# Weights of the accumulating DMAs read from HBM, a new order of the raw homes, and P2 ahead of P6 in the first pair of a chunk

## The chip, the cores and the metric

The kernel runs on one NeuronCore of a Trainium2 chip. The metric is the time of one execution on the device in microseconds (us), median over runs; the time before is 2619.73 us.

## The reference, cut to what matters

The reference is one step of a two-layer decoder on 512 prompt positions and 64 sample positions, 576 token columns in all. Each layer is a half-step SwiGLU FFN, a mixer (convolution, spatial gating, windowed attention, joined by `w_out`), and a second half-step FFN. The change lies in the four FFNs and in the edge between a mixer and the FFN behind it:

```python
def swiglu(x, w_gu, w_down):
    gu = x @ w_gu
    return (jax.nn.silu(gu[..., :D_FF]) * gu[..., D_FF:]) @ w_down

x = x + 0.5 * swiglu(rms_norm(x, n1), gu1, dn1)
m, conv_state, k_rows, v_rows, v_gmlp = token_mixer(rms_norm(x, nm), ...)
x = x + m
x = x + 0.5 * swiglu(rms_norm(x, n2), gu2, dn2)
```

`D_MODEL` is 1024 and `D_FF` is 2816, so the gate and the up matrix of an FFN have 22 column tiles of 128 each. Everything is float32.

## The kernel before, in words

**Precision.** Each weight block and each activation is split in a high part `h` (rounded to fp32r by a copy on ACT) and a rest `lo` = block - `h`. A product is three matmuls per 128 rows: `h` by high, `h` by low, `lo` by high. One matmul is 128x128 by 288 columns (half of the 576 tokens).

**A pair.** Column tile j of the gate and column tile j of the up matrix form a pair. It is computed from 2x2 blocks (`a11`, `a12` of the gate, `a21`, `a22` of the up matrix, each 128 x 512 numbers, 256 KB) by seven products instead of eight. The items of a pair are, by their number q in the code: 0 is P1 with `a11`, 1 is P5 with s0 = a21 + a22, 3 is P6 with s1 = s0 - a11, 2 is P2 with `a12`, 4 is P7 with s2 = a21 - a11, 5 is P3 with s3 = a12 - s1, 6 is P4 with `a22`. The four sums are made on DVE (`combine`, tile `sums`). A product has 12 matmuls (`product`, L563). P1, P6, P7 and P4 write the PSUM tile `c` (names `m` and `n` in turn), the others `z`. Behind P6 DVE adds `c` to a kept P5 (`z<-n,p`, L613), behind P7 it does so again (`u<-n,p`, L621); the next product that writes the same `c` waits for that read.

**Chunks.** An FFN works through its 22 pairs in four chunks; behind each chunk stand the down-projection matmuls of its pairs (`plain_ff` items, weights `w_dn`). The first pair of a chunk runs P1, P5, P6, P2 without work of an earlier pair between; in the later pairs the end of the pair before (P7, P3, P4) is mixed in. In the very first FFN three pairs are computed in plain form, so 85 pairs are left, in 16 chunks.

**The weight pipeline.** `load_raw` (L221) issues the load of a raw block on SP's queue, in order, into the next *raw home*: a list of ten homes (L227) is taken in rotation. `wr` has 4 buffers, `cb` has 4, `vT` and `ws` one each; tiles in `cb`, `vT` and `ws` carry the name `wc` in the rows. The mixer uses the `cb`, `vT` and `ws` storage for its own tiles, `cb` up to the last tile of `w_out`. A load waits until the block that had the home before has been read for the last time. `prepare` (L271) makes `h` and `lo` in a form buffer (eight, so the preparation of item i waits until PE has finished item i - 8); `advance` (L301) keeps the preparation seven items ahead of PE and the loads six items ahead of that. There are two ways. `by_vector` (L257): ACT copies `h`, DVE subtracts. `by_dma` (L263), used for `a11`, `a12` and `a22`, 255 times in all:

```python
        se.activation(out=h, in_=src, func=AF.Copy)
        se.activation(out=lo, in_=src, func=AF.Copy, scale=-1.0)
        ge.dma_start(out=lo.bitcast(F32), in_=src, accum_op=ALU.add)
```

Here ACT writes `h` and minus `h`, and an accumulating DMA, issued by POOL, adds the raw tile `src` to the second, so that `lo` = block - `h` without DVE. The raw tile is read by that DMA, and its home stays taken until the DMA has landed.

The order of the instructions on each engine is set by a scheduler when the program is built; at run time each engine's queue goes in order.

Of the kernel before, what the change touches and what calls it, by code (L numbers as in the profile page):

```python
# [9 lines left out]
F32 = mybir.dt.float32  # L10
F32R = mybir.dt.float32r
I32 = mybir.dt.int32
AF = mybir.ActivationFunctionType
ALU = mybir.AluOpType
# [81 lines left out]
def trunk(ctx: ExitStack, tc: tile.TileContext, a):  # L96
# [3 lines left out]
    ve, se, ge, sy = (_At(tc, e, HI) for e in (nc.vector, nc.scalar, nc.gpsimd, nc.sync))  # L100
# [29 lines left out]
    def ztile():  # L130
        return zp.tile([P, 2, 512], F32, tag="z", name="z")
# [30 lines left out]
    items = []  # L162

    def plain(ap, n, kind="plain", n0=0):
        for k0 in range(n0, n, 4):
            items.append((kind, ap[:, k0:min(k0 + 4, n), :], min(n - k0, 4)))

    def chunks(l, f):
        return CHUNKS0 if l == 0 and f == 0 else CHUNKS

    def ffn_items(l, f):
        j0 = N_PLAIN if l == 0 and f == 0 else 0
        gu = a["w_gu"][l, f]
        for j in range(j0):
            if j == 0:
                for n in (4, 8):
                    for h in range(2):
                        plain(gu[h], n, "plain_ff", n - 4)
            else:
                for h in range(2):  # L180
                    plain(gu[2 * j + h], 8, "plain_ff")
        for k0, k1 in chunks(l, f):
            last = None
            for j in range(max(k0, j0), k1):
                for i, q in ((j, 0), (j, 1)) if last is None else ((j, 1), (last, 4), (j, 0), (last, 5), (last, 6)):
                    items.append(("pair", (l, f, i), q))
                for q in (3, 2):
                    items.append(("pair", (l, f, j), q))
                last = j
            dn = [a["w_dn"][l, f, m, :, k0:k1, :] for m in range(KD)]  # L190
            for q in (4, 5):
                items.append(("pair", (l, f, last), q))
            plain(dn[0], 4, "plain_ff")
            items.append(("pair", (l, f, last), 6))
            plain(dn[1], 4, "plain_ff")
            plain(dn[0], k1 - k0, "plain_ff", 4)
            plain(dn[1], k1 - k0, "plain_ff", 4)
            for m in range(2, KD):
                plain(dn[m], k1 - k0, "plain_ff")
# [17 lines left out]
    state = {"load": 0, "prep": 0, "use": 0}  # L217
    state["form"] = state["raw"] = 0
    raws, ready = {}, {}

    def load_raw(i):  # L221
        kind, what, n = items[i]

        def raw(key, ap, n):
            home = "wr"
            if kind in ("pair", "plain_ff"):
                home = ("wr", "vT", "wr", "ws", "wr", "cb", "wr", "cb", "cb", "cb")[state["raw"] % 10]  # L227
                state["raw"] += 1
            if home == "wr":
                t = wp.tile([P, 4 * P], F32, tag="wr", name="wr", bufs=4)  # L230
            elif home == "cb":
                t = sp.tile([P, CB], F32, tag="cb", name="wc", bufs=4)
            else:
                t = sp.tile([P, 640 if home == "vT" else 768], F32, tag=home, name="wc")
            t = t[:, 0:n * P].rearrange("p (k m) -> p k m", k=n)
            sy.dma_start(out=t, in_=ap)
            raws[key] = t

        if kind != "pair":
            raw(i, what, n)  # L240
        else:
            l, f, j = what
            for h, k in {0: ((0, 0),), 1: ((1, 0), (1, 4)), 2: ((0, 4),)}.get(n, ()):
                raw((what, h, k), a["w_gu"][l, f, 2 * j + h, :, k:k + 4, :], 4)

    def parts(ff, n):
        tag = "w"
        if ff:
            tag = ("sp", "w", "pt", "w")[state["form"] % 4]
            state["form"] += 1  # L250
        if tag == "w":
            f = wp.tile([P, 2, 4, P], F32R, tag="w", name="w", bufs=4)
        else:
            f = big(tag, "w", F32R).rearrange("p (a k m) -> p a k m", a=2, k=4)
        return f[:, 0, 0:n, :], f[:, 1, 0:n, :]
# [4 lines left out]
        ve.tensor_tensor(out=lo, in0=src, in1=h.bitcast(F32), op=ALU.subtract)  # L260
        return h, lo, n

    def by_dma(src, n):  # L263

        h, lo = parts(True, n)
        se.activation(out=h, in_=src, func=AF.Copy)
        se.activation(out=lo, in_=src, func=AF.Copy, scale=-1.0)
        ge.dma_start(out=lo.bitcast(F32), in_=src, accum_op=ALU.add)
        return h, lo, n

    def prepare(i):  # L271
        kind, what, n = items[i]
        if kind != "pair":
            ready[i] = by_vector(raws.pop(i), n, kind != "plain")
            return

        a11, a12, a21, a22 = (raws.get((what, h, k)) for h, k in ((0, 0), (0, 4), (1, 0), (1, 4)))
        s = state["sums"]

        def combine(q, x, y, op):  # L280
            ve.tensor_tensor(out=s[:, q], in0=x, in1=y, op=op)

        if n == 0:
            r = by_dma(a11, 4)
        elif n == 1:
            combine(0, a21, a22, ALU.add)
            r = by_vector(s[:, 0], 4)
        elif n == 3:
            combine(1, s[:, 0], a11, ALU.subtract)
            r = by_vector(s[:, 1], 4)  # L290
            combine(2, a21, a11, ALU.subtract)
        elif n == 2:
            r = by_dma(a12, 4)
            combine(3, a12, s[:, 1], ALU.subtract)
        elif n == 6:
            r = by_dma(a22, 4)
        else:
            r = by_vector(s[:, n - 2], 4)
        ready[what, n] = r
# [273 lines left out]
    def ffn(l, f, nxt):  # L573
        start = l == 0 and f == 0
        p5s = slot("e", "p5").rearrange("p (i n) -> p i n", i=2)
        r = None
        for k0, k1 in chunks(l, f):
# [32 lines left out]
            def p6(o):  # L610

                product(o["c"], weights(o["what"], 3), fac["b"][3], False)
                ve.tensor_tensor(out=o["z"][:, 1, h1], in0=o["c"], in1=o["p5"], op=ALU.add)  # L613

            def p2(o):
                product(o["z"][:, 0, h1], weights(o["what"], 2), fac["b"][2], False)
# [54 lines left out]
            last = None  # L671
            for j in range(k0, k1):
                if start and j < N_PLAIN:
                    plainly(j)
                    continue
                o = {"what": (l, f, j), "z": ztile(), "c": mtile("n" if j % 2 else "m")[:, h1], "p5": p5s[:, j % 2, h1]}
                if last is None:
                    p1(o)
                    p5(o)
                    seed(o)  # L680
                    save(o)
                else:
                    p5(o)
                    save(o)
                    p7(last)
                    p1(o)
                    seed(o)
                    p3(last)
                    p4(last)
                p6(o)  # L690
                p2(o)
                if r is None:
                    r = rms()
                last = o
# [575 lines left out]
```

## Time and profile before

| | us |
|---|---|
| median of 3 runs | 2619.73 (2618.04 to 2623.62) |
| profiled execution, its own time | 2623.66 |
| profiled execution, span from first to last instruction | 2621.9 |
| PE busy | 2584.4 (99%) |
| DVE busy | 1909.9 (73%) |
| ACT busy | 1273.5 (49%) |
| POOL busy | 286.9 (11%) |

The mean granted TensorE clock of the span is 0.995. The DMA queues moved 303.30 MB, of it 66.86 MB by the accumulating DMAs of POOL; HBM read is 221.43 MB, 88 GB/s over the span.

How to read it: busy time of PE includes the overlap of pipelined matmuls, so a stretch in which PE is busy throughout is one in which a matmul starts every 132 ns; the number of matmuls in a stretch tells how much of it was lost. An engine's instructions go in order, so one that waits holds all that stand behind it.

### The profile page before, as it was taken

To read this page: it belongs to the slowest core of one execution; us is meant where nothing else is said; L and a number is where in the kernel's file an instruction comes from. 1 tells how busy PE (TensorE), PEld (TensorE's weight loads), DVE (VectorE), ACT (ScalarE), POOL (GpSimd) and SP (SyncE) were. 2 spreads that over 40 slices of the span, in tenths; PEclk is the share of its full clock that TensorE was granted. 3 is DMA by queue.
4 is the path that set the end of the run, shared out by engine and by line. 5 is a ranking of instruction groups with operands and counts; after the bars stand their busy time and mean duration, and the time that the engine had idled before them with its cause. 6 is when DMAs were issued, how large, how long until landed. Compare 5 with 4: busy or idle time off the path is not lost.

```text
span 2621.9 us, 49387 instructions
## 1 busy us (share of the span) xinstructions
PE 2584.4 (99%) x18996; PEld 2519.7 (96%) x18996; DVE 1909.9 (73%) x3488; ACT 1273.5 (49%) x2415; POOL 286.9 (11%) x317
## 2 busy tenths in 40 slices
PE   8999999999999999999999999999999999999999
PEld 8999999988899999999999999998989999999999
DVE  8676665688897786766885766747988977756665
ACT  6455453335424564554674554532453245644543
POOL 0111010010010021111110111101100100111110
PEclk9999999999999999999999999999999999999999
DMA  6565454231222464655564655533212234655553
GB/s 178 129 147 130 123 121 129 84 88 58 67 83 81 131 151 124 147 124 131 132 136 119 149 125 132 141 103 85 78 57 73 85 104 123 142 126 137 126 135 95
DMA packets 193920, 303.30 MB, mean 116 GB/s; under 512 B 39434, under 2 KB 56714, under 8 KB 193684
## 3 DMA queue, kind: packets, MB, share of 16 engines
q1 hardware_dynamic: 156820, 233.28, 29.5%
q0 software_dynamic: 36720, 66.86, 15.2%
q8 instruction: 149, 2.44, 0.4%
q14 instruction: 87, 0.71, 0.1%
q10 hardware_dynamic: 144, 0.00, 0.0%
HBM read 221.43 MB, written 8.84 MB: 88 GB/s over the span
## 4 chain that ended last, share of the span: by engine, by line
PE 91%; DVE 3%; DMA 3%; issue 1%; ACT 1%; SPq 0%; POOL 0%; DVEq 0%; POOLq 0%; ACTq 0%
PE z L322 18%; PE z L325 17%; PE z L328 17%; PE z L569 14%; PE n L569 9%; PE m L569 9%; PE n L86 4%; PE m L86 2%; DMA wc<-w_gu 2%; DMA w<-wc 1%; DVE w L88 1%; ACT w L88 1%; DVE u L88 0%; DVE sums L88 0%; DVE x L88 0%
## 5 line engine op out<-in xcount | busy, mean ns | idle before, releaser
L88 ACT ACTIVATE w<-wr 128x512 fp32r<-128x512 f32 (+1 forms) x533 | 324.0, 622 | 657.9 <-PE z L328 526.2
L569 PE MATMUL z<-xh,w 128*128 128x288 f32 x2040 | 443.4, 299 | 5.5 <-DVE z L88 3.7
L88 ACT ACTIVATE w<-wc 128x512 fp32r<-128x512 f32 (+2 forms) x509 | 271.5, 565 | 243.3 <-PE z L328 89.1
L88 DVE TENSOR_TENSOR w<-sums,w 128x512 fp32r<-128x512 f32 x340 | 234.1, 689 | 198.5 <-ACT w L88 194.7
L569 PEld LDWEIGHTS z<-xh,w 128*128 128x128 f32 x2040 | 337.5, 188 | 11.8 <-DVE z L88 5.8
L322 PE MATMUL z<-xh,w 128*128 128x288 f32 x1520 | 337.4, 303 | 8.0 <-ACT w L88 6.6
L88 DVE TENSOR_TENSOR w<-wr,w 128x512 fp32r<-128x512 f32 (+2 forms) x373 | 254.3, 682 | 122.0 <-ACT w L88 121.5
L325 PE MATMUL z<-xl,w 128*128 128x288 f32 x1520 | 328.0, 297 | 0.0
L328 PE MATMUL z<-xh,w 128*128 128x288 f32 x1520 | 327.7, 296 | 0.0
L322 PE MATMUL z<-ah,w 128*128 128x288 f32 x1408 | 303.6, 296 | 0.4
L325 PE MATMUL z<-al,w 128*128 128x288 f32 x1408 | 302.1, 296 | 0.6 <-DVE al L88 0.5
L328 PE MATMUL z<-ah,w 128*128 128x288 f32 x1408 | 301.3, 296 | 0.0
L569 PE MATMUL z<-xl,w 128*128 128x288 f32 x1020 | 300.5, 295 | 0.0
L88 ACT ACTIVATE w<-sums 128x512 fp32r<-128x512 f32 x340 | 212.1, 624 | 176.3 <-PE z L569 90.4
L322 PEld LDWEIGHTS z<-xh,w 128*128 128x128 f32 x1520 | 245.6, 191 | 22.1 <-issue 11.7
L325 PEld LDWEIGHTS z<-xl,w 128*128 128x128 f32 x1520 | 248.2, 191 | 0.7 <-issue 0.7
L328 PEld LDWEIGHTS z<-xh,w 128*128 128x128 f32 x1520 | 246.7, 190 | 0.5 <-issue 0.3
L88 DVE SCALAR_TENSOR_TENSOR c<-cb,vec,c 128x512 f32<-128x512 f32 x480 | 244.5, 556 | 0.2
L322 PEld LDWEIGHTS z<-ah,w 128*128 128x128 f32 x1408 | 226.7, 189 | 2.6 <-DVE x L88 2.3
L325 PEld LDWEIGHTS z<-al,w 128*128 128x128 f32 x1408 | 226.6, 189 | 1.8 <-DVE al L88 1.8
L328 PEld LDWEIGHTS z<-ah,w 128*128 128x128 f32 x1408 | 226.6, 189 | 0.0
L88 POOL DMA_DIRECT2D w<-wc x175 | 150.5, 860 | 616.6 <-ACT w L88 221.3
(255 smaller groups left out, 4854.5 us busy)
## 6 DMA issues: line engine op xcount, KB each, us to landing
wc<-w_gu SPq DMA_DIRECT2D x212, 256.0 KB, 2.9
wr<-w_in SPq DMA_DIRECT2D x184, 256.0 KB, 2.8
w<-wc POOLq DMA_DIRECT2D x175, 256.0 KB, 3.7
wr<-w_gu SPq DMA_DIRECT2D x140, 256.0 KB, 2.8
wr<-w_dn SPq DMA_DIRECT2D x92, 256.0 KB, 2.8
w<-wr POOLq DMA_DIRECT2D x80, 256.0 KB, 4.1
wc<-w_dn SPq DMA_DIRECT2D x36, 256.0 KB, 3.0
wr<-w_out SPq DMA_DIRECT2D x32, 256.0 KB, 3.2
```

Source lines behind the costliest of these rows:

```text
L86: r = f(*args, **kw)
L88: r = f(*args, **kw)
L322: pe.matmul(out=z[c], lhsT=wh, rhs=rh[:, s], start=first, stop=False)
L325: pe.matmul(out=z[c], lhsT=wh, rhs=rl[:, s], start=False, stop=False)
L328: e = pe.matmul(out=z[c], lhsT=wl, rhs=rh[:, s], start=False, stop=last)
L569: e = pe.matmul(out=out, lhsT=w[:, k, :], rhs=r, start=first and k == 0 and i == 0, stop=k == n - 1 and i == 2, skip_group_check=True)
```

## The change

Three things, and one that follows from them.

1. `by_dma` gets a third argument, the block in HBM, and the accumulating DMA reads that instead of the raw tile. The raw tile is then read by the two ACT copies (and by `combine`), no longer by the DMA.
2. The list of raw homes has two `wr` in positions 4 and 5 and the four `cb` at its end, and the rotation starts again at each `w_out` tile of a mixer, so that the FFN behind a mixer begins with `wr`, `vT`, `wr`, `ws`, `wr`, `wr`.
3. In the first pair of a chunk P2 comes ahead of P6, in the list of items and in the program; s3 is made in the preparation of P6 (item 3) instead of P2 (item 2). `a12` is loaded with item 3 in the later pairs, an item earlier than before. In the first pair of a chunk the key of the load list is 2 for the item behind P5 and 3 for the other, so the condition holds for both: `a12` is loaded twice there, 16 loads of 256 KB more on SP's queue in the whole program (P2's two copies read the later one).

```diff
@@ -184,7 +184,7 @@
             for j in range(max(k0, j0), k1):
                 for i, q in ((j, 0), (j, 1)) if last is None else ((j, 1), (last, 4), (j, 0), (last, 5), (last, 6)):
                     items.append(("pair", (l, f, i), q))
-                for q in (3, 2):
+                for q in (2, 3) if last is None else (3, 2):
                     items.append(("pair", (l, f, j), q))
                 last = j
             dn = [a["w_dn"][l, f, m, :, k0:k1, :] for m in range(KD)]
@@ -218,13 +218,17 @@
     state["form"] = state["raw"] = 0
     raws, ready = {}, {}
 
+    def block(what, h, k):
+        l, f, j = what
+        return a["w_gu"][l, f, 2 * j + h, :, k:k + 4, :]
+
     def load_raw(i):
         kind, what, n = items[i]
 
         def raw(key, ap, n):
             home = "wr"
             if kind in ("pair", "plain_ff"):
-                home = ("wr", "vT", "wr", "ws", "wr", "cb", "wr", "cb", "cb", "cb")[state["raw"] % 10]
+                home = ("wr", "vT", "wr", "ws", "wr", "wr", "cb", "cb", "cb", "cb")[state["raw"] % 10]
                 state["raw"] += 1
             if home == "wr":
                 t = wp.tile([P, 4 * P], F32, tag="wr", name="wr", bufs=4)
@@ -236,12 +240,13 @@
             sy.dma_start(out=t, in_=ap)
             raws[key] = t
 
+        if kind == "plain_out":
+            state["raw"] = 0
         if kind != "pair":
             raw(i, what, n)
         else:
-            l, f, j = what
-            for h, k in {0: ((0, 0),), 1: ((1, 0), (1, 4)), 2: ((0, 4),)}.get(n, ()):
-                raw((what, h, k), a["w_gu"][l, f, 2 * j + h, :, k:k + 4, :], 4)
+            for h, k in {0: ((0, 0),), 1: ((1, 0), (1, 4)), (2 if items[i - 1][2] == 1 else 3): ((0, 4),)}.get(n, ()):
+                raw((what, h, k), block(what, h, k), 4)
 
     def parts(ff, n):
         tag = "w"
@@ -260,12 +265,12 @@
         ve.tensor_tensor(out=lo, in0=src, in1=h.bitcast(F32), op=ALU.subtract)
         return h, lo, n
 
-    def by_dma(src, n):
+    def by_dma(src, n, hbm):
 
         h, lo = parts(True, n)
         se.activation(out=h, in_=src, func=AF.Copy)
         se.activation(out=lo, in_=src, func=AF.Copy, scale=-1.0)
-        ge.dma_start(out=lo.bitcast(F32), in_=src, accum_op=ALU.add)
+        ge.dma_start(out=lo, in_=hbm.bitcast(F32R), accum_op=ALU.add)
         return h, lo, n
 
     def prepare(i):
@@ -281,7 +286,7 @@
             ve.tensor_tensor(out=s[:, q], in0=x, in1=y, op=op)
 
         if n == 0:
-            r = by_dma(a11, 4)
+            r = by_dma(a11, 4, block(what, 0, 0))
         elif n == 1:
             combine(0, a21, a22, ALU.add)
             r = by_vector(s[:, 0], 4)
@@ -289,11 +294,11 @@
             combine(1, s[:, 0], a11, ALU.subtract)
             r = by_vector(s[:, 1], 4)
             combine(2, a21, a11, ALU.subtract)
+            combine(3, a12, s[:, 1], ALU.subtract)
         elif n == 2:
-            r = by_dma(a12, 4)
-            combine(3, a12, s[:, 1], ALU.subtract)
+            r = by_dma(a12, 4, block(what, 0, 4))
         elif n == 6:
-            r = by_dma(a22, 4)
+            r = by_dma(a22, 4, block(what, 1, 4))
         else:
             r = by_vector(s[:, n - 2], 4)
         ready[what, n] = r
@@ -687,8 +692,12 @@
                     seed(o)
                     p3(last)
                     p4(last)
-                p6(o)
-                p2(o)
+                if last is None:
+                    p2(o)
+                    p6(o)
+                else:
+                    p6(o)
+                    p2(o)
                 if r is None:
                     r = rms()
                 last = o
```

On POOL the 255 accumulating DMAs, which alternated between `w<-wr` and `w<-wc`, all read `w_gu` now. Their number and their place among POOL's other work stay. Three places show what else moves.

DVE in the first pair of the third chunk of the first FFN: `sums<-...` are the four combinations, `w<-sums,w` a subtraction of `by_vector`, `z<-n,p` and `u<-n,p` the reads of `c` behind P6 and P7. Before:

```order
L88 TENSOR_TENSOR sums<-wc,sums 128x512
L88 TENSOR_TENSOR w<-sums,w 128x512
L88 TENSOR_TENSOR sums<-sums,wr 128x512
L88 TENSOR_TENSOR z<-n,p_185 128x288
L88 TENSOR_TENSOR w<-sums,w 128x512
L88 TENSOR_TENSOR sums<-wc 128x512
L88 TENSOR_TENSOR w<-sums,w 128x512
L88 TENSOR_TENSOR u<-n,p_185 128x288
```

With the change:

```order
L88 TENSOR_TENSOR sums<-wc,sums 128x512
L88 TENSOR_TENSOR w<-sums,w 128x512
L88 TENSOR_TENSOR sums<-sums,wc 128x512
L88 TENSOR_TENSOR z<-n,p_185 128x288
L88 TENSOR_TENSOR w<-sums,w 128x512
L88 TENSOR_TENSOR sums<-wc,wr 128x512
L88 TENSOR_TENSOR w<-sums,w 128x512
L88 TENSOR_TENSOR u<-n,p_185 128x288
```

The combination that stands ahead of `u<-n,p` is the first sum of a later pair in both; its two raw blocks lay in two `wc` homes, now in a `wc` (the `vT` home) and a `wr`.

SP at the start of the last FFN, behind the mixer of the second layer: the last loads of `w_out`, then the FFN's own. Before:

```order
L88 DMA wr<-w_out 128x512 x4
L88 DMA wr<-w_gu 128x512 x4
L88 DMA wc<-w_gu 128x512 x5
L88 DMA wr<-w_gu 128x512
L88 DMA wc<-w_gu 128x512
L88 DMA wr<-w_gu 128x512 x2
L88 DMA wc<-w_gu 128x512 x2
L88 DMA wr<-w_gu 128x512 x2
```

With the change:

```order
L88 DMA wr<-w_out 128x512 x4
L88 DMA wr<-w_gu 128x512 x3
L88 DMA wc<-w_gu 128x512
L88 DMA wr<-w_gu 128x512 x3
L88 DMA wc<-w_gu 128x512 x4
L88 DMA wr<-w_gu 128x512
L88 DMA wc<-w_gu 128x512
L88 DMA wr<-w_gu 128x512
```

Four loads for `wr` and five for `wc` (the first of them into `cb`) stood in a row; now three for `wr`, one for `wc` (the `vT` home), three for `wr` and then four for `wc`.

PE in the first pair of a chunk, from the end of P6 to the start of P7 (`n<-fh` and `n<-fl` are both; the `z` rows between are other products). Before, in which 9 more `z` rows follow ahead of the first `n<-fh` of P7:

```order
L569 MATMUL n<-fh,w 128x288
L569 MATMUL z<-xl_81,w 128x288
L569 MATMUL z<-xh_73,w 128x288
L569 MATMUL z<-xh_74,w 128x288
L569 MATMUL z<-xl_82,w 128x288
L569 MATMUL z<-xh_74,w 128x288
L569 MATMUL z<-xh_75,w 128x288
L569 MATMUL z<-xh_76,w 128x288
L569 MATMUL z<-xl_84,w 128x288
L569 MATMUL z<-xh_76,w 128x288
L569 MATMUL z<-xh_77,w 128x288
L569 MATMUL z<-xl_85,w 128x288
```

With the change, up to the start of P7:

```order
L574 MATMUL n<-fh,w 128x288
L574 MATMUL z<-xl_81,w 128x288
L574 MATMUL z<-xh_73,w 128x288
L574 MATMUL z<-xh_74,w 128x288
L574 MATMUL z<-xl_82,w 128x288
L574 MATMUL z<-xh_74,w 128x288
L574 MATMUL z<-xh_75,w 128x288
L574 MATMUL z<-xl_83,w 128x288
L574 MATMUL z<-xh_75,w 128x288
L574 MATMUL n<-fh,w 128x288
```

Between the last matmul of P6 and the first of P7 stood 20 matmuls, now 8; the 12 of P2 stand between the two halves of P6 instead.

## Rows read from the trace of the kernel before

**Rows 1.** What PE waited for in the whole span: total us, times, longest.

```profile
PE z L569 <- DVE z L88: 3.7, 8, 0.6
...
PE m L569 <- ACT z L88: 1.2, 1, 1.2
```

**Rows 2.** What SP's queue waited for in the whole span: total us, times, longest.

```profile
SPq L88 <- DMA w<-wc: 532.3, 173, 11.1
SPq L88 <- DMA w<-wr: 322.5, 77, 10.6
```

**Rows 3.** Stretches: PE, PEld, DVE, ACT, POOL busy (instructions); granted clock, DMA share, GB/s.

```profile
260.00:300.00 40.00, 40.00 (x303) 39.89 (x302) 28.30 (x50) 19.90 (x37) 3.44 (x4) 1.00 0.56 142
...
217.00:240.00 23.00, 22.17 (x163) 21.45 (x163) 14.09 (x24) 13.64 (x26) 5.16 (x6) 1.00 0.67 145
326.00:345.00 19.00, 17.26 (x116) 16.77 (x116) 10.62 (x20) 9.81 (x19) 3.44 (x4) 0.91 0.68 142
920.00:944.00 24.00, 22.00 (x161) 20.89 (x161) 20.66 (x48) 16.56 (x34) 5.19 (x7) 1.00 0.64 153
...
2212.00:2242.00 30.00, 25.54 (x184) 24.02 (x183) 25.82 (x57) 20.33 (x40) 5.99 (x7) 1.00 0.66 163
2340.00:2351.00 11.00, 10.16 (x75) 9.69 (x74) 8.68 (x16) 6.62 (x12) 2.58 (x3) 1.00 0.75 166
2448.00:2459.00 11.00, 10.09 (x74) 9.62 (x73) 8.44 (x15) 6.43 (x12) 2.58 (x3) 1.00 0.74 168
```

**Rows 4.** Chain that ended last, third chunk's start: start us, us, what.

```profile
220.76 4.68 DMA w<-wc
225.50 3.60 DMA wc<-w_gu
```

**Rows 5.** DVE's timeline there: start, us, instruction, [idle before <- releaser].

```profile
223.28 0.47 DVE L88 TENSOR_TENSOR z<-n,p 128x288 f32<-128x288 f32 x1
226.35 0.69 DVE L88 TENSOR_TENSOR w<-sums,w 128x512 fp32r<-128x512 f32 x1 [2.60 <-ACT w L88]
229.18 0.69 DVE L88 TENSOR_TENSOR sums<-wc 128x512 f32<-128x512 f32 x1 [2.14 <-DMA wc<-w_gu]
...
230.39 0.45 DVE L88 TENSOR_TENSOR u<-n,p 128x288 f32<-128x288 f32 x1
```

**Rows 6.** ACT's timeline there, the two copies of `a22`.

```profile
219.31 1.15 ACT L88 ACTIVATE w<-wc 128x512 fp32r<-128x512 f32 x2 [0.93 <-PE n L569]
```

**Rows 7.** PE's timeline there: P6's end, P7's start, P4's start.

```profile
222.88 0.29 PE L569 MATMUL n<-fh,w 128*128 128x288 f32 x1
...
225.75 0.29 PE L569 MATMUL n<-fh,w 128*128 128x288 f32 x1
...
230.90 0.66 PE L569 MATMUL n<-f,w 128*128 128x288 f32 x3 [0.23 <-DVE u L88]
```

**Rows 8.** Chain that ended last, fourth chunk's start.

```profile
327.92 4.66 DMA w<-wc
...
332.64 5.15 DMA wc<-w_gu
...
339.58 2.41 PE n L569 x12
```

**Rows 9.** DVE's timeline there.

```profile
337.87 0.69 DVE L88 TENSOR_TENSOR sums<-wc 128x512 f32<-128x512 f32 x1 [3.66 <-DMA wc<-w_gu]
```

**Rows 10.** SP's and PE's timelines at the last FFN's start.

```profile
2210.64 5.10 SPq L88 DMA_DIRECT2D wc<-w_gu  x5
...
2221.11 0.40 PE L569 MATMUL n<-xh,w 128*128 128x288 f32 x1 [1.48 <-ACT w L88]
...
2225.53 0.54 PE L569 MATMUL n<-xh,w 128*128 128x288 f32 x2 [1.46 <-DMA w<-wr]
```

**Rows 11.** DVE's timeline at the start of the FFN behind the first mixer.

```profile
920.30 0.69 DVE L88 TENSOR_TENSOR sums<-wr,wc 128x512 f32<-128x512 f32 x1 [1.25 <-DMA wc<-w_gu]
```

**Rows 12.** DMA issues by the page: KB each, median us from issue to landing.

```profile
wc<-w_gu SPq DMA_DIRECT2D x212, 256.0 KB, 2.9
...
w<-wc POOLq DMA_DIRECT2D x175, 256.0 KB, 3.7
```

## The prediction

> **What bounds the kernel now.** I begin with the stretches [rows 3]. In the undisturbed one, from 260 to 300 us, PE starts 303 matmuls in 40.00 us, one each 0.132 us, while DVE (28.30 us) and ACT (19.90 us) have room. That is the bound for nearly the whole span, and no part of this change takes a matmul away: the time can fall only by what PE stands still. How much a stretch loses is its length less its matmuls times 0.132 us. From 217 to 240 us that is 23.00 - 163 x 0.132 = 1.48 us, from 326 to 345 us 19.00 - 116 x 0.132 = 3.69 us, from 2340 to 2351 us 1.10 us, from 2448 to 2459 us 1.23 us, and at the starts of the two FFNs behind a mixer 2.75 us (920 to 944) and 5.71 us (2212 to 2242). These six places together are 15.96 us, some 0.6% of the time; the edges of a stretch make each uncertain by a matmul.
>
> Next, who makes PE wait at a chunk's start. The chain of waits of the third chunk [rows 4] has the accumulating DMA from 220.76 us for 4.68 us, and behind it at once, at 225.50 us, a load of the next raw blocks for 3.60 us. DVE's timeline [rows 5] shows what hangs on it: the combination that needs those blocks starts at 229.18 us after 2.14 us of waiting, and `u<-n,p`, which needs nothing of it but stands behind it, only at 230.39 us. P4 writes the `c` that this reads, so PE starts it at 230.90 us [rows 7]. The load waited for a home that the accumulating DMA was still reading, though ACT had made both its copies from 219.31 us in 1.15 us [rows 6]. The fourth chunk repeats it a size larger: accumulation 4.66 us, load 5.15 us [rows 8], DVE waits 3.66 us [rows 9], and then P4 takes 2.41 us for its 12 matmuls instead of 12 x 0.132 = 1.58, under a mean granted clock of 0.91 in that stretch [rows 3], which is a part of it at 1.2 instead of 2.4 GHz after PE had stood still. In the whole span SP's queue waited 532.3 and 322.5 us for accumulating DMAs [rows 2]; little of that reaches PE, but PE's waits for DVE's `z` sum to 3.7 us in 8 places [rows 1], at just these starts.
>
> **The change part by part.** *The DMA reads HBM.* A home comes free when ACT has copied: at 219.31 + 1.15 = 220.46 us, where it was 225.50 us, some 5.0 us earlier. The load then lands near 220.5 + 3.6 = 224.1 us, and the combination, which stands behind a subtraction that ends at 226.35 + 0.69 = 227.04 us [rows 5], finds its blocks there. `u<-n,p` can then start when P7 has ended, 12 matmuls after 225.75 us [rows 7], near 227.7 us, well before P4's turn. What is late next is the subtraction that waits for ACT, 2.60 us at 226.35 us [rows 5], but it is over before P7 ends. So the four starts go: 1.48 + 3.69 + 1.10 + 1.23 = 7.5 us, the half clock included; two smaller ones of the kind I leave out. I take 7.4 of it, bounds 4 (only the waits that DVE is named for [rows 1, 7]) and 8.
>
> The accumulating DMA itself: the trace has none with HBM as its source. Its price lies between that of a plain load, 2.9 us, and 3.7 us plus the 2.25 us that a slowed load took more (5.15 against 2.9) [rows 8, 12]. I take 3.7, as before, since it moves as many bytes into the same tile. The one at 220.76 us landed at 225.44 us and PE used its form at 230.90 us: 5.4 us to spare, so neither end reaches PE in the steady work. The cover fails only at the first products of an FFN.
>
> The Trainium skill speaks against this part: its page "HBM Reference", section "Latency", gives 0.2 us for an access on average and 2 us under high load. By that page, as an estimate, an accumulation would land up to 2 us later than from on-chip memory; no run here shows it yet. It would add 2 us at each of the two places where an accumulation holds PE at an FFN's start, so the sum below would be 4 us smaller.
>
> *The homes.* Behind the mixer the first pair had its blocks in `cb` homes that the mixer held to its end: the load row at 2210.64 us is 5.10 us long for five issues [rows 10], and DVE waits 1.25 us for such a load at 920.30 us [rows 11]. Now the first six blocks have `wr`, `vT` and `ws`. Of the last FFN's loss of 5.71 us the 1.48 us at 2221.11 us and the 1.46 us at 2225.53 us [rows 10] go, and of the rest (the DVE that has fallen behind) I count 1.1 us: 4.0. Of the first layer's 2.75 us I count 1.3, by the ACT wait of 1.2 us [rows 1] that follows on the DVE wait. The rest of both belongs to the residual stream's own preparation and stays. Together 5.3, bounds 0 and 8.46. The FFNs that stand behind another FFN or at the program's beginning get no earlier homes: 0.
>
> *P2 ahead of P6.* DVE's `z<-n,p` starts 0.40 us after the start of P6's last matmul (222.88 to 223.28 us [rows 5, 7]), and PE could use `c` some 0.51 us later (230.39 to 230.90 us, the same kind of read). So P7 may follow 0.91 us after that start. With 20 matmuls between it came 21 x 0.132 = 2.77 us later, with 8 it comes 1.19 us later: 0.28 us is left. A DVE instruction of 0.69 us in front of it would cost 0.41 us, at most 6.6 us over 16 first pairs; where DVE is idle, as here, nothing. I take 1.0 us. That P2 and the load of `a12` move by an item costs nothing: seven items of look-ahead cover it.
>
> *The second load of `a12`.* 16 more loads of 2.9 us [rows 12] on a queue that waits hundreds of microseconds anyway: 0, with 16 x 0.33 us of issue as the worst, off PE's path.
>
> *The program's beginning.* The scheduler sets a subtraction of 0.69 us ahead of a small chain that PE waits for in the first FFN's normalisation. I take 1.0 us of loss, bounds 0 and 1.4 (two of them).
>
> Sum: -7.4 - 5.3 + 1.0 + 1.0 = -10.7 us. From the profiled execution's 2623.66 us that is 2613.0; this execution stands 3.9 us above the median of the runs, so the median comes to 2609 us. With the bounds of the terms the likeliest case reaches from about 2602 (-16.5 us of gain, no loss, and some scatter of the runs) to 2616 (gains of 4 and 3, losses of 1.4 and 2).
>
> **The rivals.** *The earlier loads collide.* Loads that are freed by ACT's copies start within a microsecond or two of POOL's accumulating DMA; the row of 5.15 us shows a load stretched by such company [rows 8]. At the fourth chunk it would still land at 327.9 + 5.15 = 333.1 us, ahead of the 337.87 - 3.66 = 334.2 us at which DVE wanted it, so the chunk starts keep their gain. The FFN starts, where the loads come one behind the other, would not: 5.3 us are lost again, 2614.3 us. The Trainium skill, "DMA: Bandwidth & Descriptors", section "Issuing engines are not separate DMA queues", says that transfers of sync and gpsimd run on the same 16 engines and interleave; this trace agrees with it by that row.
>
> *Accumulations from HBM land later.* Were they later by the 2.25 us of the stretched load, two FFN starts would pay it: 4.5 us, 2613.6 us. For it: nothing but the longer way. Against it: the loads, which come from HBM, land sooner (2.9 us) than the accumulations (3.7 us) [rows 12].
>
> *Slower: DVE is late for P7.* If the combinations go on waiting for loads, now in front of `z<-n,p`, then a wait such as the 2.14 us [rows 5] no longer lies under 20 matmuls: P7 starts 2.14 - 0.28 = 1.86 us late at 16 first pairs, 29.8 us, against 10.7 of gain: 2638.8 us. It decides against the change once DVE is late by about 1.3 us on average (16 x 1.0 us = 10.7 + 5.3). Against it: DVE had been idle at that point in the rows, for some 2 us on each side.
>
> *The waits only change their name.* DVE's queue stands behind another late block or subtraction at the same starts; then PE gains nothing it can keep, 2619.7 us.
>
> **How the numbers follow.** The likeliest case has 0.60, the later accumulations 0.10, the collision 0.12, DVE late for P7 0.09, waits that only change their name 0.09. About 0.2%, 5.2 us, is what a measurement of this kernel can tell from no change: faster means below 2614.5, slower above 2625.0. The collision, at 2614.3, counts half. Faster: 0.60 + 0.10 + 0.06 = 0.76; same 0.06 + 0.09 = 0.15; slower 0.09. The range goes from 2602 to 2618: it leaves out the two last rivals, 0.18, and takes in the others with their scatter.
>
> **What would show it.** In the profile of the changed kernel SP's queue should no longer wait for accumulating DMAs. At the third and fourth chunk's start DVE should start its combination without waiting for a load, `u<-n,p` right behind P7, and the granted clock from 326 to 345 us should be 1.00. The matmuls counted in the six stretches should come out at 0.132 us each, except for some 1.5 us at each FFN behind a mixer. The forecast is wrong if `w<-w_gu` takes over 5.9 us to land, if PE waits at P7 for DVE's `z` at many chunk starts, or if the loads behind the mixer still begin late.

## The result, and the profile after

The changed kernel takes 2603.64 us (median of 4 runs, 2601.36 to 2607.47), the kernel before 2620.32 us beside it (4 runs, 2618.04 to 2623.62): a ratio of 0.9937, 95% interval 0.9920 to 0.9954. The forecast was 2609 us, range 2602 to 2618. Run a second time beside other kernels, the same program took 2606.52 us against 2619.44, ratio 0.9951 (0.9938 to 0.9963), so the gain lies near 13 to 17 us. The profiled execution took 2607.47 us; its span is 2605.7 us, 16.2 us less than that of before. What is read from HBM rises from 221.43 to 292.47 MB, 116 GB/s over the span.

The same seven stretches as in [rows 3], moved by as much as their place in the program had moved, in the profile of the changed kernel (PE, PEld, DVE, ACT and POOL busy with their instructions, granted clock, DMA share, GB/s):

```profile
260.00:300.00 40.00, 40.00 (x302) 39.83 (x301) 29.10 (x51) 20.20 (x38) 4.31 (x5) 1.00 0.57 135
219.70:242.70 23.00, 23.00 (x174) 22.77 (x173) 15.67 (x27) 14.63 (x28) 5.17 (x6) 1.00 0.72 157
327.40:346.40 19.00, 19.00 (x143) 18.77 (x142) 12.41 (x22) 11.89 (x24) 4.32 (x5) 1.00 0.77 164
916.00:940.00 24.00, 23.40 (x174) 22.61 (x173) 20.98 (x49) 17.19 (x34) 5.17 (x6) 1.00 0.67 148
2200.40:2230.40 30.00, 29.58 (x221) 28.78 (x220) 25.84 (x57) 20.56 (x40) 5.14 (x6) 1.00 0.58 140
2327.70:2338.70 11.00, 11.00 (x85) 10.97 (x84) 8.54 (x16) 6.93 (x14) 2.59 (x3) 1.00 0.87 175
2434.30:2445.30 11.00, 11.00 (x84) 10.97 (x84) 8.50 (x16) 7.41 (x14) 2.59 (x3) 1.00 0.84 179
```

Where PE stood still before it now starts a matmul every 0.132 us: 174 in 23.00 us (163 before), 143 in 19.00 us (116), 85 and 84 in 11.00 us (75 and 74), all at a granted clock of 1.00, also in the stretch that had 0.91. The starts behind a mixer lose 24.00 - 174 x 0.132 = 1.03 us and 30.00 - 221 x 0.132 = 0.83 us where it was 2.75 and 5.71.

SP's queue waits, summed over the span of the changed kernel (total us, times, longest):

```profile
SPq L88 <- DVE w L88: 943.4, 445, 5.5
SPq L88 <- ACT w L88: 493.4, 210, 9.7
SPq L88 <- DVE sums L88: 360.8, 85, 15.7
```

No accumulating DMA is left among them [rows 2]; ACT's copies and DVE's combinations release the homes. DVE's timeline in the first pair of the third chunk shows what follows [rows 5]:

```profile
227.62 0.47 DVE L88 TENSOR_TENSOR z<-n,p 128x288 f32<-128x288 f32 x1 [1.66 <-PE n L574]
228.46 0.69 DVE L88 TENSOR_TENSOR w<-sums,w 128x512 fp32r<-128x512 f32 x1 [0.37 <-ACT w L88]
229.18 0.69 DVE L88 TENSOR_TENSOR sums<-wc,wr 128x512 f32<-128x512 f32 x1
229.79 0.68 DVE L88 TENSOR_TENSOR w<-sums,w 128x512 fp32r<-128x512 f32 x1
230.39 0.45 DVE L88 TENSOR_TENSOR u<-n,p 128x288 f32<-128x288 f32 x1
```

The combination at 229.18 us waits for no load, and `u<-n,p` stands right behind the end of P7. PE's and SP's timelines beside it:

```profile
227.22 0.29 PE L574 MATMUL n<-fh,w 128*128 128x288 f32 x1
...
228.41 0.30 PE L574 MATMUL n<-fh,w 128*128 128x288 f32 x1
...
2203.16 2.72 SPq L88 DMA_DIRECT2D wc<-w_gu  x4
```

The first two are P6's last matmul and P7's first: 1.19 us apart, and DVE's read of `c` began 0.40 us after the one and was over before the other, as worked out ahead. The third is the last FFN's loads into `cb`: four issues in 2.72 us at 2203.16 us, which no first product needs any more [rows 10].

Where the 16.2 us of span came from is read from DVE's 144 instructions `x<-z,x`, which end every chunk and every mixer. Between them the span falls into pieces that have the same work in all kernels of this study. "Start" is up to the end of the very first chunk, "chunks" are the other 15 up to their last `x<-z,x`, "FFN behind mixer" runs from a mixer's first `x<-z,x` to its last (the first pair of the next FFN lies in it), "attention" runs from the first to the last gate product `gz<-z,rstd` of a mixer, and the rest of the mixers is alike in all to 0.3 us. Each column is the difference to the profile of before, in us:

| profiled kernel | start | 15 chunks | FFN behind mixer | attention |
|---|---|---|---|---|
| the change | +3.47 | -10.67 | -5.16 | -3.68 |
| the change, once more | +2.58 | -12.06 | -5.20 | -3.32 |
| HBM as source alone | +0.64 | -8.43 | -0.23 | -6.14 |
| raw homes alone | -1.70 | -1.57 | -6.81 | -5.42 |
| P2 ahead of P6 alone | +1.06 | -1.76 | +3.30 | -5.78 |
| a12 loaded once | +0.79 | -10.61 | -6.80 | -6.31 |
| HBM source, home held | -0.66 | +9.77 | -0.46 | -3.39 |
| HBM source and homes | +3.40 | -11.95 | -6.80 | -3.05 |
| old order in first chunk | +1.86 | -12.95 | -6.80 | -5.65 |
| old order in first chunks | +3.52 | -12.61 | -6.79 | -4.54 |
| source and homes, tile at start | +1.29 | -12.87 | -6.80 | -3.94 |
| old order and tile at start | -1.52 | -10.09 | -6.81 | -4.05 |

The column "FFN behind mixer" repeats to 0.1 us between kernels that share the homes and have no second load of `a12`; "chunks" lies between -10.1 and -13.0 us in all eight profiles with source and homes. "Attention" does not repeat, and it is lower in every other profile, though none of the kernels changes the mixers' code. It is a property of the one execution, most of all of the profiled one of before, which stood 3.9 us above its median.

A good part of what does not repeat in "start" and "chunks" is TensorE's granted clock. In the profile of before it is below 1.00 once in the 15 chunks, in the fourth chunk, in the stretch that [rows 3] give with 0.91:

```profile
338.00:348.00 10.00, 8.42 (x52) 8.42 (x53) 8.42 (x15) 4.31 (x8) 1.72 (x2) 0.83 0.69 160
```

Ten us at 0.83 are a part at 1.2 instead of 2.4 GHz; they lose up to 10 x (1 - 0.83) = 1.7 us of matmuls, as an estimate (counted in matmuls, two such places below lose 1.3 and 1.5 us). The profile with the homes alone has the same fall at the same place, both of the change have one in the third FFN instead, several have none in the chunks, and that with the home held has three. Without these stretches (at 1.7 us each, so roughly) the eight profiles with source and homes lie at -10.1 to -12.1 us in the chunks, HBM alone at -8.4, the homes alone at -1.6, the order alone at -0.1 and the held home at +6.4.

### The profile page after: what moved, and what is told of

Read it like the earlier page. It is cut to its first block, busy times and chain, and to the rows that moved or that the text cites. A ratio compares the mean times of both kernels' runs of the same rounds, so it can differ in the third digit from the quotient of the medians.

```text
span 2605.7 us, 49108 instructions
## 1 busy us (share of the span) xinstructions
PE 2577.6 (99%) x18996; PEld 2519.0 (97%) x18996; DVE 1910.9 (73%) x3488; ACT 1272.8 (49%) x2415; POOL 291.3 (11%) x317
## 3 DMA queue, kind: packets, MB, share of 16 engines
HBM read 292.47 MB, written 8.84 MB: 116 GB/s over the span
## 4 chain that ended last, share of the span: by engine, by line
PE 94%; DVE 3%; DMA 1%; ACT 1%; issue 1%; POOL 0%; SPq 0%; DVEq 0%; POOLq 0%; ACTq 0%
PE z L327 18%; PE z L330 17%; PE z L333 17%; PE z L574 15%; PE n L574 10%; PE m L574 10%; PE n L86 4%; PE m L86 2%; DVE w L88 1%; ACT w L88 0%; DVE x L88 0%; DMA rt<-q 0%; DMA wr<-w_gu 0%; DVE c L88 0%; DVE sums L88 0%
## 5 line engine op out<-in xcount | busy, mean ns | idle before, releaser
L88 ACT ACTIVATE w<-wr 128x512 fp32r<-128x512 f32 (+2 forms) x575 | 337.8, 604 | 625.7 <-PE z L333 487.7
L88 ACT ACTIVATE w<-wc 128x512 fp32r<-128x512 f32 (+2 forms) x467 | 257.8, 583 | 303.2 <-PE z L333 133.1
L88 POOL DMA_DIRECT2D w<-w_gu x255 | 220.2, 864 | 1507.3 <-ACT w L88 980.7
L88 DVE TENSOR_TENSOR w<-wr,w 128x512 fp32r<-128x512 f32 (+2 forms) x373 | 240.6, 645 | 82.6 <-ACT w L88 81.6
L327 PEld LDWEIGHTS z<-xh,w 128*128 128x128 f32 x1520 | 245.5, 191 | 22.2 <-issue 11.7
```

Source lines behind the costliest of these rows:

```text
L88: r = f(*args, **kw)
L327: pe.matmul(out=z[c], lhsT=wh, rhs=rh[:, s], start=first, stop=False)
```

## The experiments

**HBM as the source alone.** Accumulating DMAs as in the change, everything else as before.

```diff
+    def block(what, h, k):
...
-        ge.dma_start(out=lo.bitcast(F32), in_=src, accum_op=ALU.add)
+        ge.dma_start(out=lo, in_=hbm.bitcast(F32R), accum_op=ALU.add)
```

> Only the accumulating DMAs read HBM; raw homes, products and loads as before. Theory (a home is released by ACT's copies instead of the landing): the waits of DVE at the chunk starts near 229, 337, 2344 and 2451 us go, the two FFNs behind a mixer still begin late; gain 7 to 11 us, 2609 to 2613 us. Rival (the order of P2 and P6 makes the chunk starts' gain): 2618 to 2621 us. Rival (the way to HBM costs where little is to spare): landing over 4 us and PE waiting for an accumulation at FFN starts, gain under 5 us.

Measured: 2613.91 us against 2621.37, ratio 0.9973 (0.9964 to 0.9983), and -8.43 us in the 15 chunks, nothing at the FFNs behind a mixer. The theory holds for the chunk starts, though the time lies 0.9 us above its range: on DVE no combination waits longer than 0.9 us for a load any more, and the pieces that hold the four places give 1.99, 3.53, 1.35 and 1.61 us. Nor was it the scheduler's order: with operation and tile names side by side, PE and POOL run the same sequence as before, and DVE and ACT differ only by the place of two instructions and of one, all within the first 40 us; on SP four transfers or groups of them stand elsewhere, none of them at the four places. The rival on the landing holds too, in a small way: an accumulation takes 4.6 us to land from HBM, and PE waits for it at three places (PE's waits, total us, times, longest):

```profile
PE n L573 <- DMA w<-w_gu: 3.3, 2, 2.2
PE m L573 <- DMA w<-w_gu: 2.0, 1, 2.0
```

Before, these were 1.5 and 1.0 us.

**The raw homes alone.** The list and its new start at each `w_out` tile.

```diff
-                home = ("wr", "vT", "wr", "ws", "wr", "cb", "wr", "cb", "cb", "cb")[state["raw"] % 10]
+                home = ("wr", "vT", "wr", "ws", "wr", "wr", "cb", "cb", "cb", "cb")[state["raw"] % 10]
...
+        if kind == "plain_out":
+            state["raw"] = 0
```

> Only the list of raw homes and its new start at each tile of w_out; the accumulating DMAs read the raw tile, products as before. Theory: the two FFNs behind a mixer gain 5 to 7 us together, the chunk starts go on waiting for loads behind accumulations (perhaps at other chunks): 2613 to 2617 us. Rival (the early homes are worth little without the earlier release): 2618 to 2621 us.

Measured: 2609.15 us, ratio 0.9959 (0.9946 to 0.9971), more than either theory gave. Of the pieces -6.81 us lie at the FFNs behind a mixer, as expected; -1.57 us in the chunks, where the waits only move to others, and the rest in the start (where the clock of this profile stayed at 1.00) and in attention, the pieces that scatter. The rival falls: the early homes do not need the earlier release.

**P2 ahead of P6 alone.**

```diff
-                for q in (3, 2):
+                for q in (2, 3) if last is None else (3, 2):
...
-            for h, k in {0: ((0, 0),), 1: ((1, 0), (1, 4)), 2: ((0, 4),)}.get(n, ()):
+            for h, k in {0: ((0, 0),), 1: ((1, 0), (1, 4)), (2 if items[i - 1][2] == 1 else 3): ((0, 4),)}.get(n, ()):
...
+                if last is None:
+                    p2(o)
+                    p6(o)
```

> Only P2 ahead of P6 in a chunk's first pair, the third combination in P6's preparation, a12 loaded with P6 (twice in first pairs). Theory: it gives nothing by itself, 2619 to 2623 us, with DVE still waiting for loads at chunk starts. Rival (it makes the gain at the chunk starts): 2608 to 2614 us. Rival (P7 waits for DVE's read of c): over 2625 us, with waits of PE for DVE z at many first pairs.

Measured: 2621.91 us against 2621.37, ratio 1.0011 (1.0000 to 1.0022): nothing, as the theory said. No `<- DVE z` stands against `m` or `n` in PE's waits, so P7 never waited for the read of `c`; only waits of `z` do, somewhat more than before [rows 1]. The first row is PE's, the second from SP's timeline:

```profile
PE z L569 <- DVE z L88: 5.8, 11, 0.6
...
2210.01 8.28 SPq L88 DMA_DIRECT2D wc<-w_gu  x6
```

The second is the last FFN's loads behind the mixer: six issues in 8.28 us where five took 5.10 [rows 10]. One more load waits there for a home, and the FFNs behind a mixer lose 3.30 us.

**One load of a12 in a chunk's first pair.** The change without the 16 dead loads.

```diff
-            for h, k in {0: ((0, 0),), 1: ((1, 0), (1, 4)), (2 if items[i - 1][2] == 1 else 3): ((0, 4),)}.get(n, ()):
+            for h, k in {0: ((0, 0),), 1: ((1, 0), (1, 4)), (2 if items[i - 1][2] == 1 else 7 if items[i - 1][2] == 2 else 3): ((0, 4),)}.get(n, ()):
```

> The change, but a12 is loaded once in a chunk's first pair (16 loads of 256 KB fewer). Theory (a dead load lies off PE's path): within 2 us of the change's 2603.6 us. Rival (the second load holds a home and SP's queue where little is to spare): faster by 3 us or more.

Measured: 2603.32 us, ratio 0.9936 (0.9923 to 0.9948): the change's time. In the pieces the dead load does cost, at one place: the FFNs behind a mixer take -6.80 us instead of -5.16 and -5.20, so 1.6 us of it are lost there. Elsewhere no cost of it shows: DVE's waits for loads are 15.1 and 8.1 us in the change and 4.0 and 3.7 us here (from `wc` and `wr` homes), and the chunks take the same.

**HBM as the source, the home held.** What of the chunk starts' gain is the release? Behind each accumulating DMA of the first experiment a tiny DMA reads the raw tile.

```diff
         ge.dma_start(out=lo, in_=hbm.bitcast(F32R), accum_op=ALU.add)
+        late = tp.tile([P, 1], F32, tag="late", name="late", bufs=4)
+        with tc.issue_after(e.ins):
+            ge.dma_start(out=late, in_=src[:, 0, 0:1])
```

> The accumulating DMAs read HBM and nothing else of the change, but behind each a DMA of four bytes per partition reads the raw tile, so that its home stays taken for some 3 us more. Theory (the chunk starts gain by the earlier release alone): DVE waits for loads at the chunk starts near 229, 337, 2344 and 2451 us again, and the 8.4 us that the chunks of the run with HBM as the only change gave are lost: 2617 to 2624 us. Rival (the source itself does it, or the order that the scheduler then chose): 2609 to 2616 us.

Measured: 2627.63 us against 2621.15, ratio 1.0028 (1.0016 to 1.0039), some 14 us above the run without the tiny DMA. That is outside the theory's range, on the far side from the rival. SP's queue waits for the tiny DMA as it had waited for the accumulations, and DVE for the loads behind it (first two rows SP's, then DVE's in total and its timeline at the third and fourth chunk's start; the last from the DMA issues, KB each, median us to landing):

```profile
SPq L88 <- DMA late<-wc: 541.4, 173, 12.1
SPq L88 <- DMA late<-wr: 356.5, 77, 11.1
...
DVE sums L88 <- DMA wc<-w_gu: 29.0, 23, 4.1
...
230.29 0.69 DVE L88 TENSOR_TENSOR sums<-wc 128x512 f32<-128x512 f32 x1 [2.58 <-DMA wc<-w_gu]
...
336.57 0.69 DVE L88 TENSOR_TENSOR sums<-wc 128x512 f32<-128x512 f32 x1 [1.23 <-DMA wc<-w_gu]
...
late<-wc POOLq DMA_DIRECT2D x175, 0.5 KB, 4.1
```

DVE's row in the run with HBM alone:

```profile
DVE sums L88 <- DMA wc<-w_gu: 6.2, 15, 0.9
```

The chunks lose 9.77 us against before, where they had gained 8.43. At all four places DVE waits for a load again (2.58, 1.23, 2.70 and 2.76 us), and 3.95 and 4.12 us at two chunk starts of the second FFN, where it had waited under 1.0 us and 1.17 us before. The loss is more than the theory's return to before: the tiny DMA is issued 0.55 us behind the other (221.42 and 221.97 us on POOL) and takes 4.1 us, 4.7 us in all, so it holds the home longer than the accumulation from the tile did (3.7 us), and behind the two longest waits the granted clock is 0.83 for 10 us besides. PE, DVE, ACT and, but for the tiny DMAs, POOL run the very sequence of before; on SP eleven of 1017 transfers stand elsewhere. PE's waits for accumulations are 3.6 and 1.8 us where they were 3.3 and 2.0 with HBM alone, so the extra issues do not delay these. The release makes the gain; the source itself and the order do not. Place by place the sum does not carry over: the fourth chunk, where the wait is shorter than before and the clock 1.00, still gains 3.11 us.

**HBM source and homes, without the order and the second load.** The first two experiments' edits together.

```diff
-        ge.dma_start(out=lo.bitcast(F32), in_=src, accum_op=ALU.add)
+        ge.dma_start(out=lo, in_=hbm.bitcast(F32R), accum_op=ALU.add)
...
+                home = ("wr", "vT", "wr", "ws", "wr", "wr", "cb", "cb", "cb", "cb")[state["raw"] % 10]
...
+            state["raw"] = 0
```

> HBM as the source and the new raw homes with their new start, without the new order of P2 and P6 and without the second load of a12. Theory (the two parts remove the same kind of wait at different places, and the order gives nothing): the chunk starts and the starts behind a mixer are both clean, and the program's beginning stays as before: 2598 to 2603 us, not slower than the change. Rival (the order is needed beside them): 2607 us or more.

Measured: 2605.44 us, ratio 0.9947 (0.9934 to 0.9959), between theory and rival, beside the change's 2606.52 on the same chip. Chunks -11.95 and FFN behind mixer -6.80: both clean, without P2 ahead of P6. What it misses of the theory is the start, +3.40 us, which the last experiment takes up.

**The old order in the very first chunk, and in every first chunk** (each with one load of a12).

```diff
-                for q in (2, 3) if last is None else (3, 2):
+                for q in (2, 3) if last is None and (l, f, k0) != (0, 0, 0) else (3, 2):
...
+                for q in (2, 3) if last is None and k0 != 0 else (3, 2):
```

The second line is that of the other kernel.

> The change with a12 loaded once, but P6 ahead of P2 in the program's very first chunk. Theory (the loss of some 3 us at the beginning comes from the new order there, which sets DVE's subtractions ahead of the normalisation): the beginning as before or better, 2599 to 2602 us. Rival (it comes from the accumulation's later landing): 2603 us or more.

> The change with a12 loaded once, but P6 ahead of P2 in the first chunk of every FFN. Theory: besides the beginning the third FFN's start gets back 1.2 us: 2598 to 2601 us. Rival (that start lost by the homes or by the source): as with the very first chunk alone.

Measured: 2601.82 us, ratio 0.9933 (0.9920 to 0.9947), in its theory's range, and 2604.18 us, ratio 0.9940 (0.9928 to 0.9953), 3.2 us above its own; not told apart. The start scatters (+1.86 and +3.52 us with the same program up to there), so the order is not what loses it.

The second kernel's theory on the third FFN fails by the first kernel. That FFN's first chunk is 1.22 to 1.27 us slower than before in four profiles with the new order there (both of the change, a12 loaded once, old order and tile at start), but within 0.1 us of before in the two others that have the new order there, the order alone and the first kernel here. Ten us of that chunk in the change, and the same ten in the first kernel here:

```profile
1320.00:1330.00 10.00, 9.41 (x59) 9.20 (x60) 7.53 (x21) 5.31 (x12) 0.96 (x2) 0.83 0.45 107
```

```profile
1316.54:1326.54 10.00, 9.42 (x69) 9.01 (x70) 8.77 (x25) 6.08 (x13) 1.51 (x3) 1.00 0.44 108
```

PE is busy for as long in both, after the same two stops of 0.8 us at the start of the stretch, but at a granted clock of 0.83 it fits 59 matmuls in and at 1.00 it fits 69. DVE is late there for the next `z`, behind the normalisation's small instructions (`no`), in all six:

```profile
PE z L574 <- DVE no L88: 1.1, 1, 1.1
```

This row is in the change and, word for word, in the first kernel, whose chunk loses nothing by it against the old order with its other stops. So the 1.2 us are the clock's and not DVE's. Whether the new order's stops make the fall likelier stays open: four of six profiles with the new order there have it, none of the seven with the old one.

**The change once more.**

> The change itself once more, to stand beside the others on the same chip: 2602 to 2606 us; the stretch at the start of each mixer's attention scatters by some 3 us between executions of kernels that leave it alone, and should again differ from the first profile.

Measured: 2606.52 us (2605.47 to 2609.03), half a us above the range. The scatter shows within one program. The same stretch of the second layer's attention, first in the change's first profile, then in this one:

```profile
1825.00:1835.00 10.00, 10.00 (x74) 9.78 (x75) 10.00 (x18) 5.68 (x10) 6.04 (x3) 1.00 0.37 101
```

```profile
1825.00:1835.00 10.00, 10.00 (x58) 9.82 (x58) 8.83 (x13) 5.62 (x10) 3.10 (x4) 0.72 0.40 115
```

PE stood still just ahead of it in both (matmuls start 1.98 and 1.95 us apart there). Behind the pause the granted clock was 1.00 once, and 0.72 the other time, a part at 1.2 instead of 2.4 GHz, and 74 matmuls fitted in 10 us or 58.

**The raw tile as the source in the very first chunk**, with source and homes alone, and with the old order in the first chunk.

```diff
+    def source(what, h, k):
+        l, f, j = what
+        return None if l == f == 0 and j < CHUNKS0[0][1] else block(what, h, k)
...
+        if hbm is None:
+            ge.dma_start(out=lo.bitcast(F32), in_=src, accum_op=ALU.add)
+        else:
             ge.dma_start(out=lo, in_=hbm.bitcast(F32R), accum_op=ALU.add)
```

> HBM source and new homes without the new order, but the accumulating DMAs of the program's very first chunk read the raw tile. Theory (the landing from HBM, some 0.8 us later, costs where PE already waits for an accumulation, near 55 us): the wait falls back from 2.3 to 1.3 us and the first chunk ends 1 to 5 us earlier than with HBM there: 2600 to 2604 us. Rival (the beginning scatters by the clock alone): 2605 us or more, the wait unchanged.

> The change with a12 loaded once, P6 ahead of P2 in the very first chunk, and the raw tile as the source there. Theory: the best of all, 2598 to 2602 us, faster than the change by 3 us or more. Rival: no different from the one with the old order alone, 2601 to 2603 us.

Measured: 2603.03 us, ratio 0.9937 (0.9924 to 0.9951), in the theory's range, and 2604.66 us, ratio 0.9935 (0.9924 to 0.9947), above theory and rival. PE's waits in the start, with the tile as the source and with HBM (the kernel with source and homes):

```profile
PE m L582 <- DMA w<-wc: 1.0, 1, 1.0
```

```profile
PE m L575 <- DMA w<-w_gu: 2.0, 1, 2.0
```

The wait falls from 2.0 to 1.0 us, and the starts are at +1.29 and -1.52 us instead of +3.40 and +1.86: 2.1 and 3.4 us in the two pairs. So the landing from HBM costs 1.0 us there directly. More comes with it, as the 12 us around and behind that wait show, with the tile and with HBM:

```profile
55.00:67.00 12.00, 9.71 (x68) 8.80 (x67) 10.36 (x20) 9.02 (x19) 2.73 (x4) 1.00 0.56 105
```

```profile
55.00:67.00 12.00, 9.49 (x58) 9.01 (x57) 9.27 (x19) 7.66 (x16) 2.16 (x3) 0.86 0.62 112
```

Behind the longer stop the next 22 matmuls start within 4.4 us instead of 2.9, at a lower clock. The fall is in six of the eight profiles whose first chunk reads HBM (not in those with a12 loaded once and with the home held) and in none of the five whose first chunk reads the tile. That the longer wait brings it on is likely by this, but not shown. The rest of the difference is another stretch of lower clock, ahead of that wait, which scatters whatever the source: from 30 to 42 us the granted clock is 1.00, 0.86 or 0.72, and the 158 matmuls between the normalisation and the wait then start within 20.9, 22.2 to 22.4 or 23.0 to 23.5 us.

Of the versions with source and homes none is clearly faster than the change by the intervals, which all overlap. On one chip, though, all five runs of the kernel with one load of a12 and the old order in the very first chunk (2599.97 to 2604.82 us) lie below all five of the change's second measurement (2605.47 to 2609.03).

## Why the prediction was right, point by point

**The chunk starts** were forecast at 7.4 us, from four places. The mechanism is shown: HBM as the source alone gives 8.43 us in the chunks, and holding the home, with the same order on PE, DVE, ACT and POOL, takes it away again. The term was too small: in the change the chunks give 10.7 to 12.1 us. The four places are in it (the pieces that hold them give 1.28, 3.59, 1.39 and 1.91 us in the change's profile, 8.2 us, and 8.1 us in the second); the rest is 0.3 to 0.8 us in each of six other chunks in the first profile, 0.0 to 1.4 us in the second, among them the two smaller starts that I had left out, less some 1.25 us lost in the third FFN to the clock. The step that failed is the choice to count four places alone; those left out were a third of the chunks' gain. Not all of that third is the release: 0.8 to 1.1 us of it lie in the last FFN's first chunk, where the homes alone give 1.07 us and HBM alone loses 1.90 us, most of it to the clock.

**The FFNs behind a mixer** were forecast at 5.3 us, and 5.2 us came. That is the right number from a wrong part: the homes give 6.8 us by themselves, and the second load of `a12`, costed at nothing, takes 1.6 us of it.

**P2 ahead of P6** was given 1.0 us for P7's shorter cover. P7 never waits: 1.19 us stand between, 0.91 are needed, in the rows as in the working. No run shows a cost of the order in the chunks: alone, with the second load, it measured 1.0011 (1.0000 to 1.0022), and the 1.25 us at the third FFN's start go with the clock. So the term of 1.0 us was nothing, as far as the runs can tell.

**The accumulation from HBM** was taken at 3.7 us and bounded by 5.95. It takes 4.6 us (DMA issues by the page of the changed kernel; KB each, median us to landing):

```profile
w<-w_gu POOLq DMA_DIRECT2D x255, 256.0 KB, 4.6
wc<-w_gu SPq DMA_DIRECT2D x219, 256.0 KB, 3.0
```

This has no price in the steady work, as forecast, and one where PE already waited for an accumulation: PE's wait in the first FFN is 2.1 us in the change where it was 1.0. The rule of the Trainium skill's "HBM Reference", section "Latency", 0.2 us on average and 2 us under high load, brackets the extra 0.5 to 0.9 us (4.6 against 4.1 and 3.7), and the cost that it pointed to is there, in the change at one place instead of two and for 1.0 us instead of 2. In most profiles the slower matmuls behind it come on top, 1.5 us.

**The program's beginning** was given 1.0 us of loss, for DVE's order ahead of the normalisation. It lost 2.6 to 3.5 us, outside the bounds of 0 and 1.4. The term itself is there: DVE has two subtractions ahead of `idr`, PE waits for it, and its matmuls there start 2.04 us apart instead of 1.11. PE's waits in the change show it beside the landing from HBM, which is 1 us more:

```profile
PE m L574 <- DMA w<-w_gu: 2.1, 1, 2.1
PE m L86 <- DVE idr L532: 1.7, 1, 1.7
```

The prediction had no term for the clock, and that is most of the rest: behind the wait for the accumulation 22 matmuls take 4.4 us instead of 2.9, and the same matmuls between the normalisation and that wait took 22.4 us in the profile of before, 20.9 us in that with the homes alone and 23.0 to 23.4 us in those of the change and of source and homes, by the length of a stretch at the lower clock. Without the wait for `idr` (HBM source and homes) the start still lost 3.40 us: 1.0 by the landing, 1.5 and 1.0 by the clock at the two places, and smaller differences that nearly cancel.

**The sum.** -11.4 (chunks), -5.2, +3.0 are -13.6 us of the parts in the two profiles of the change. Against the forecast's -10.7 the chunks are the term that was mis-sized, and the start in the other direction. The first comparison of medians, 16.7 us, lies above that and the second, 12.9 us, below. So the mechanism was right, but 2603.64 us lies near the fast end of the range, and the sum came as close as it did because its errors went both ways.

The rivals: loads did not collide at the starts (the FFNs behind a mixer kept their gain), DVE was not late for P7, and the waits did not only change their name.

## What to carry to other kernels

A buffer that is still read by a slow DMA holds more than its own successor: behind it stands the in-order load queue, behind that an in-order engine, and only then the work that TensorE needs; follow such a chain to its first release and move that reader to another copy of the data, even if the transfer itself becomes longer. When such a wait is found at a few places, look for all places that share the cause before summing; the places left out were a third of the chunks' gain here. Before a difference of an us or two is put down to an order or a wait, count the matmuls of that stretch and read its granted clock in several profiles: here 1.2 us that stood beside a late DVE were the clock's.

## What the runs showed of the hardware

An accumulating DMA of 256 KB takes 4.6 to 4.7 us (median, issue to landing) with its source in HBM (4.4 us in the kernel with the held home) against 3.7 to 4.1 us from on-chip memory in the kernels where all 255 read it there, though a plain load from HBM takes 2.8 to 3.0 us. A DMA of four bytes per partition took 4.1 us to land when issued right behind such an accumulation, no less than a large one from the tile.

One program, with the same pause of 2.0 us on TensorE, ran the 10 us from 1825 us, just behind it, at a mean granted clock of 1.00 in one execution and of 0.72 in another. That alone is 2 us or more between executions, and it explains differences that no change of the kernel made. In the third FFN it fell behind two stops of 0.8 us in four profiles, and did not in two others with the same stops.
